# Head outputs of a hybrid decoder step: turned on VectorE and through HBM where they were turned on TensorE

## The chip, the cores and the metric

One core of a Trainium2 chip runs one layer of a decoder step, for a prompt of 1024 tokens (16 meta tokens ahead of it) and 8 single-token samples. The metric is the device time of one execution in microseconds. Of three runs of the kernel before, the median is 1193.43 us (1193.35 to 1194.38).

## What is computed

Cut to what matters, in the reference's names; `_chunked` runs a state through the 16 meta tokens and then through chunks of the sequence:

```python
u = _rms_norm(x, norm_w) @ w_in                       # 1024 -> 8216 columns
q_m, k_m, v_m, o_m, z_m, i_m, f_m, q_g, k_g, v_g, z_g, b_g, a_g = split(u)
(C, n, m), hm = _chunked(_mlstm_chunk, ...)           # 4 mLSTM heads, dk 128, dv 256
ym = _head_rms(hm) * w_mnorm * sigmoid(o_m) * silu(z_m)
qkv = silu(_causal_conv(conv_buf, [q_g, k_g, v_g], conv_w))
S, og = _chunked(_gdn_chunk, ...)                     # 8 gated DeltaNet heads, 128 x 128
yg = (_head_rms(og) * w_gnorm) * silu(z_g)
y = x + concatenate([ym, yg]) @ w_out                 # then a final RMSNorm
```

The same weights serve 8 samples, whose states (C, n, m, S, conv rows) are read, decayed, updated by an outer product and written back. All arithmetic is fp32 in effect: projections split each operand into a high and a low part and add three products.

## The kernel before

**Tiling.** Features lie on the 128 partitions for everything that the projections make (a tile is one head's q, k, v, or one of 8 gate tiles, over 1048 columns of tokens). The input projection takes 56 weight tiles in turn, each over three column blocks of about 350, as 8 x 3 matmuls into a PSUM bank (`pjg`, `pjm`, `pjz`, `pjo`, `pjzm` by group). These matmuls are the filler: 4720 of them, then 672 of the output projection (`op`), in a fixed order.

**Chains.** Beside the filler run the recurrent chains in chunks of 128 tokens: `gdn_chain` for heads 0 to 7, then `mlstm_chain` for heads 0 to 3. A chunk of the mLSTM chain multiplies the state (`mup`, `mnm`), lets VectorE make the next state `C` and the weighted scores `mpm`, turns the next chunk's k and v (`mtp`), and takes some one-element operations for the norm (`mst`, `hst`). Chunk outputs have tokens on the partitions: `oo` (DeltaNet) and `mho` (mLSTM) go to `h_d` in HBM, unscaled.

**Gates.** `gate(kt)` makes one of 16 tiles of the output projection's left side. It loads a head tile `ht` (8 chunks of 128 x 128, tokens on partitions), scales each chunk by the inverse root of the head norm on ScalarE, turns the chunks on TensorE (`hT`, 4 into a PSUM bank), and multiplies them into the gate tile `y` or `mg` on VectorE. DeltaNet's tiles (kt 8 to 15) go to `y_d` and `s_d`, the mLSTM's (0 to 7) are combined with them into `c_d`; the output projection is a Strassen-like scheme of 7 products that reads these as its left sides.

**Samples.** `gdn_sample` takes heads in pairs: states into `db` and `ebuf0`, products on TensorE (`sA`), a turn (`sT`), a row broadcast through HBM into `ebuf1`, decay on GpSimd (128x1024), 8 products on VectorE per head, store. `mlstm_sample` does the same per head (`mqc`, `mqT`, `mms` at the end). When both are done, `db` and the two `ebuf` are reused for the output weights (`in_wo`), summed on GpSimd and split into `owh` and `owl`.

**Order.** `Plan` is an order made while the program is written out: it keeps an estimated clock per engine, takes whichever thread can go on earliest, and otherwise issues filler. `note` holds the estimates of durations, `done`, `read` and `room` those of data, buffers and PSUM banks. Each engine then runs its instructions in exactly this order and waits where something isn't there. All DMAs of this stage are issued by one queue, SP's. Buffers come from rings (`r_kq` 3, `r_v` 4, `r_gm` 3 and later 5, `r_N` 2).

Every instruction is recorded by a helper and so has the line L56; groups are told apart by tile names.

Of the kernel before, what the change touches and what calls it, by code (L numbers as in the profile page):

```python
# [12 lines left out]
F32 = mybir.dt.float32  # L13
# [51 lines left out]
class Plan:  # L65
# [32 lines left out]

    def note(self, eng, op, out, ins, extra, power):
# [197 lines left out]
def hymba_kernel(ctx: ExitStack, tc: tile.TileContext, a: dict, o: dict):  # L297
# [158 lines left out]
    h_d = dr.tile([GH + 2 * MH, P, 8, P], F32, name="h_d")  # L456
# [589 lines left out]
    def gdn_chain(h):  # L1046
# [30 lines left out]
        for c in range(NCH):  # L1077
# [28 lines left out]
            else:  # L1106
                dve.scalar_tensor_tensor(
                    out=Sn, in0=S, scalar=egend[:, c, h : h + 1], in1=up[:, 0:P], op0=ALU.mult, op1=ALU.add)
                oo = w("oo", [258], f"oo{h}_{c}", 3)[:, 0:P]
# [3 lines left out]
                sp.dma_start(h_d[8 + h, :, c - 1, :], oo)  # L1113
# [29 lines left out]
    def query_norms():  # L1143
# [6 lines left out]
        for r in range(4):  # L1150
            rows = slice(32 * r, 32 * r + 32)
            part = pt[rows, 0 : 32 * GH].rearrange("p (h c r) -> p h c r", h=GH, r=4)[:, :, :, r]
            dve.scalar_tensor_tensor(out=hst[rows, MH : MH + GH, :], in0=part, scalar=EPS * MDK, in1=hst[rows, MH : MH + GH, :], op0=ALU.mult, op1=ALU.add)

# [10 lines left out]
    def gdn_sample():  # L1165
# [50 lines left out]
        for i in range(2):  # L1216
            sp.dma_start(sb[i], a["s_S"][i])
        for h in range(0, GH, 2):
# [52 lines left out]
            if h + 2 < GH:  # L1271
                yield plan.read[sb[1].tensor.name]
                sp.dma_start(sb[1], a["s_S"][h + 3])
        op_ = sn[:, 4]
# [11 lines left out]
    def mlstm_jobs(h):  # L1286
# [23 lines left out]
        for part in range(4):  # L1310
# [4 lines left out]
                end=(lambda: done.add(("mP", h))) if part == 3 else None)  # L1315
# [3 lines left out]
    def mlstm_chain(h):  # L1319
        yield lambda: ("mgates",) in done and r_gm.can() and r_N.can()  # L1320
        gi, ew = r_gm.get([NCH, P], f"mgm{h}")
        if h == MH - 1:
            r_gm.idle += [3, 4]
# [14 lines left out]
        yield has("mP", h)  # L1338
        (ki, kq), (v0i, v0), (v1i, v1) = hd["m", h]
        yield v1  # L1340
        qt = wq[:, 1:NCH, :].rearrange("p c t -> p (c t)")
        for c in range(0, SEQ, 512):
            pool.tensor_tensor(out=qt[:, c : c + 512], in0=qt[:, c : c + 512], in1=kq[:, 1, META + c : META + c + 512], op=ALU.mult)
        pre = {}
# [25 lines left out]
        for c in range(NCH):  # L1370
# [18 lines left out]
            if c > 0:  # L1389
                ho = w("oo", [258], f"mho{h}_{c}", 3)  # L1390
                act.copy(ho[:, 0:257], nm[:, 0:257])
                st = w("st", [4], f"mst{h}_{c}")
                jk = w("jm", [256], f"mjk{h}_{c}", bufs=1)
                act.activation(jk, ho[:, 0:256], AF.Square, scale=1.0 / 16, accum_out=st[:, 1:2])
                sp.dma_start(h_d[2 * h : 2 * h + 2, :, c - 1, :].rearrange("i t v -> t i v"), ho[:, 0:256].rearrange("p (i v) -> p i v", i=2))

                def norm(st=st, ho=ho, c=c):
                    dve.tensor_scalar(st[:, 2:3], ho[:, 256:257], -1.0, em[:, c, h : h + 1], op0=ALU.mult, op1=ALU.max)
                    dve.tensor_scalar(st[:, 0:1], ho[:, 256:257], st[:, 2:3], None, op0=ALU.max)
# [17 lines left out]
        r_kq.free(ki)  # L1417
# [5 lines left out]
    def mlstm_sample():  # L1423
# [32 lines left out]
        for h in range(MH):  # L1456
# [14 lines left out]
            for i in range(2):  # L1471
                for b in range(NS):
                    g, j = divmod(b, 4)
                    g = P * (g + 2 * i)
                    pe.matmul(qt[32 * j : 32 * j + 32, g : g + P], qf, sb[i][:, b, :], start=True, stop=True)
            vb = ebuf[1]
# [10 lines left out]
            for i in range(2):  # L1487
# [5 lines left out]
                pool.tensor_tensor(out=s_, in0=s_, in1=decb[:, h].unsqueeze(2).to_broadcast([P, NS, P]), op=ALU.mult)  # L1493
                yield s_
                yield vb
                for b in range(NS):
                    dve.scalar_tensor_tensor(out=s_[:, b], in0=vb[:, b], scalar=kw[:, h, b : b + 1], in1=s_[:, b], op0=ALU.mult, op1=ALU.add)
# [44 lines left out]
    def gate(kt_, wcol):  # L1542

        j = kt_ % 8
        if kt_ >= 8:
            yield lambda: ("mP", MH - 1) in done and ("C", j) in done and ("z", j) in done and (j in slots or (r_kq if j < 6 else r_N).can()) and r_gm.can(2)
            gi, y = r_gm.get([SEQ], f"y{kt_}")
        else:
            yield lambda: ("mC", j // 2) in done and ("y", 8 + j) in done and (j < 2 or ("y", j - 2) in done) and r_gm.can()
# [4 lines left out]
        sp.dma_start(ht, h_d[kt_])  # L1554
        hh = kt_ // 2 if kt_ < 8 else kt_ - 4
        yield has("rs", hh)
        yield rsg[hh][0]
# [3 lines left out]
        yield ht, 1.2  # L1561
# [572 lines left out]
```

## Time and profile before

| what | value |
|---|---|
| median of 3 runs | 1193.43 us |
| profiled execution | 1193.59 us, its span 1191.8 us |
| TensorE matmuls | 1175.5 us busy, 99% |
| VectorE | 880.7 us, 74% |
| ScalarE, GpSimd | 591.0 us, 459.8 us |
| HBM read, written | 107.65 MB, 45.71 MB |
| first and last `hT` | 809.0, 1022.1 us |

Times in rows are microseconds from the span's start, means and durations of single instructions nanoseconds. PE is TensorE, PEld its weight loads, DVE VectorE, ACT ScalarE, POOL GpSimd, SPq the DMA issues of SP's queue. A row of a table of stages gives for each engine its busy time and, in brackets, its instructions. Matmuls overlap in the pipeline: their busy times add up to more than the time from start to start.

### The profile page before, as it was taken

How to read it: one execution, taken by the hardware profiler on the slowest of the kernel's cores; microseconds unless marked ns; L12 is line 12 of the kernel's file. 1: busy time of each engine (PE TensorE's matmuls, PEld its weight loads, DVE VectorE, ACT ScalarE, POOL GpSimd, SP SyncE). 2: the span in 40 equal slices, each digit the busy share in tenths (PEclk: the TensorE clock that was granted, in tenths of full speed). 3: DMA queues.
4: the chain of work that ended last, by engine and by line, in shares of the span. 5: the costliest groups of instructions: out<-in, count | busy, mean ns of one | idle time of the engine just before them, and what ended most of it. 6: DMA issues, size and time to landing. Idle time of an engine off the chain costs nothing.

```text
span 1191.8 us, 22942 instructions
## 1 busy us (share of the span) xinstructions
PE 1175.5 (99%) x8248; PEld 1100.6 (92%) x8248; DVE 880.7 (74%) x2248; ACT 591.0 (50%) x1789; POOL 459.8 (39%) x640
## 2 busy tenths in 40 slices
PE   8999999999999999999999999999999999999997
PEld 7999999999999999999998989999999999876885
DVE  6789788687889888784348666637766765887886
ACT  6554445655565556554444443436444433343544
POOL 3105877837568665847004133140011111440012
PEclk9999999999999999999999999999999999999999
DMA  6032212212211212121122425355798986674342
GB/s 244 19 97 77 86 50 81 89 44 88 79 53 37 92 56 89 38 60 52 50 68 89 141 93 180 99 174 191 243 334 266 322 304 233 214 281 130 108 159 89
DMA packets 87084, 154.86 MB, mean 130 GB/s; under 512 B 26793, under 2 KB 48513, under 8 KB 86970
## 3 DMA queue, kind: packets, MB, share of 16 engines
q1 hardware_dynamic: 86776, 153.23, 38.9%
q8 instruction: 65, 1.06, 0.4%
q14 instruction: 49, 0.40, 0.1%
q10 hardware_dynamic: 194, 0.17, 0.0%
HBM read 107.65 MB, written 45.71 MB: 129 GB/s over the span
## 4 chain that ended last, share of the span: by engine, by line
PE 90%; DVE 5%; DMA 1%; issue 1%; ACT 1%; POOL 1%; SPq 0%; DVEq 0%; POOLq 0%; ACTq 0%
PE pjg L56 23%; PE pjm L56 13%; PE op L56 9%; PE pjo L56 8%; PE pjzm L56 8%; PE pjz L56 7%; PE up L56 4%; PE tp L56 3%; PE sk L56 2%; PE mnm L56 2%; PE mup L56 2%; PE hT L56 1%; PE kk L56 1%; PE mtp L56 1%; PE E L56 1%
## 5 line engine op out<-in xcount | busy, mean ns | idle before, releaser
L56 PE MATMUL pjg<-xht,whg 128*128 128x350 f32 (+6 forms) x624 | 197.4, 323 | 1.0 <-ACT xht L56 1.0
L56 PE MATMUL pjg<-xlt,whg 128*128 128x350 f32 (+6 forms) x624 | 197.4, 323 | 0.0
L56 PE MATMUL pjg<-xht,wlg 128*128 128x350 f32 (+6 forms) x592 | 190.5, 325 | 0.0
L56 POOL TENSOR_TENSOR tmp<-B,E 33x31 f32<-33x31 f32 (+15 forms) x248 | 147.8, 596 | 70.7 <-DMA B<-nd 51.9
L56 POOL TENSOR_TENSOR E<-E,tmp 33x31 f32<-33x31 f32 (+15 forms) x248 | 153.5, 619 | 19.5
L56 PE MATMUL op<-owh,left 128*128 128x512 f32 x448 | 141.6, 395 | 0.7 <-DVE xr L56 0.7
L56 PE MATMUL pjm<-xht,wlm 128*128 128x350 f32 (+2 forms) x384 | 126.4, 329 | 0.6 <-DVE wlm L56 0.6
L56 PE MATMUL pjm<-xht,whm 128*128 128x350 f32 (+2 forms) x384 | 126.5, 329 | 0.0
L56 PE MATMUL pjm<-xlt,whm 128*128 128x350 f32 (+2 forms) x384 | 125.8, 328 | 0.0
L56 PEld LDWEIGHTS pjg<-xht,whg 128*128 128x128 f32 x624 | 116.4, 189 | 1.9 <-issue 1.2
L56 PEld LDWEIGHTS pjg<-xlt,whg 128*128 128x128 f32 x624 | 116.4, 189 | 0.3
L56 PEld LDWEIGHTS pjg<-xht,wlg 128*128 128x128 f32 x592 | 110.9, 189 | 0.5
L56 PEld LDWEIGHTS op<-owh,left 128*128 128x128 f32 x448 | 84.1, 188 | 22.5 <-issue 1.7
L56 DVE SCALAR_TENSOR_TENSOR kq<-cr,prm,kq 128x346 f32<-128x346 f32 (+7 forms) x147 | 94.0, 646 | 11.3 <-ACT kq L56 8.0
L56 POOL TENSOR_TENSOR db<-db,sgb 128x1024 f32<-128x1024 f32 x8 | 15.9, 1985 | 189.9 <-PE mqc L56 121.4
L56 PE MATMUL op<-owl,left 128*128 128x512 f32 x224 | 88.3, 394 | 0.0
L56 PEld LDWEIGHTS pjm<-xht,wlm 128*128 128x128 f32 x384 | 72.5, 189 | 1.4 <-DVE wlm L56 1.2
L56 PEld LDWEIGHTS pjm<-xlt,whm 128*128 128x128 f32 x384 | 72.4, 188 | 0.5 <-issue 0.2
L56 PEld LDWEIGHTS pjm<-xht,whm 128*128 128x128 f32 x384 | 72.3, 188 | 0.4
L56 POOL TENSOR_TENSOR mwq<-mt,mgm 128x384 f32<-128x384 f32 x12 | 10.7, 888 | 140.0 <-DVE mgm L56 140.0
L56 PE MATMUL pjz<-xht,whz 128*128 128x344 f32 x192 | 62.8, 327 | 0.0
L56 ACT COPY cr<-pjg 128x3 f32<-128x3 f32 (+8 forms) x124 | 40.5, 326 | 44.9 <-PE pjg L56 44.6
(368 smaller groups left out, 3211.0 us busy)
## 6 DMA issues: line engine op xcount, KB each, us to landing
wrg<-in_wt SPq DMA_DIRECT2D x23, 512.0 KB
left<-c_d SPq DMA_DIRECT2D x40, 256.0 KB
wrm<-in_wt SPq DMA_DIRECT2D x16, 512.0 KB
ht<-h_d SPq DMA_DIRECT2D x16, 512.0 KB
gm<-rows_d SPq DMA_DIRECT2D x8, 576.0 KB
xt<-in_x_p SPq DMA_DIRECT2D x8, 512.0 KB
wrz<-in_wt SPq DMA_DIRECT2D x8, 512.0 KB
h_d<-oo SPq DMA_DIRECT2D x64, 64.0 KB
```

Source lines behind the costliest of these rows:

```text
L56: r = f(*args, **kw)
```

## The change

1. **Turning.** `oo` goes to a buffer of its own, `o_d`. The new `turns` reads a DeltaNet head back once the DeltaNet norms are there, scales it on ScalarE, and `store` turns it on VectorE in 32x32 blocks (4 instructions of 128x256) and writes it to `h_d` in 4 DMAs of 32 partitions, which put the blocks where a full transpose has them. An mLSTM chunk's output stays in SBUF, in the place of the q and k that it has used up (`mkq`); `stores` takes the inverse roots with a power on GpSimd, scales on ScalarE and calls `store` for the head's two halves. `h_d` now holds scaled tiles with features on partitions, up to an order of columns; `gate` loads one and multiplies it in 4 pieces (128x8x32), without TensorE and without scalings.
2. **Weights.** `mlstm_weights` is a thread of its own: decays and scores' weights of a head are made once the DeltaNet inverses are done and q is there, ahead of the chain.
3. **Samples.** The decay on GpSimd is issued right behind `sA` or `mqc`; the second row broadcast has a buffer (`svb`) of its own; the products yield to other VectorE work after every second one.
4. **Estimates** of VectorE's transpose, reduce and memset in `note` are raised.

```diff
@@ note @@
-            cost = 0.07 + n * (1.04e-3 if len(ins) > ptr + (op[0] == "s") or op == "transpose" else 0.6e-3)
-            cost += 0.06 * ptr
+            if op in ("transpose", "tensor_reduce"):
+                n, cost = free(ins[0]), 1.55e-3
+            else:
+                cost = 1.04e-3 if len(ins) > ptr + (op[0] == "s") else 1.15e-3 if op == "memset" else 0.6e-3
+            cost = 0.07 + n * cost + 0.06 * ptr
...
-    h_d = dr.tile([GH + 2 * MH, P, 8, P], F32, name="h_d")
+    o_d = dr.tile([GH, P, 8, P], F32, name="o_d")
+    h_d = dr.tile([2 * MH + GH, P, D], F32, name="h_d")
...
+    def store(k, o_):
+        yield r_gm.can
+        ti, turn = r_gm.get([D], f"turn{k}")
+        yield plan.read[turn.tensor.name]
+        for b in range(4):
+            yield "dve"
+            blocks = o_.rearrange("p (c b j) -> p b c j", c=8, b=4)[:, b]
+            dve.transpose(turn[:, 256 * b : 256 * b + 256].rearrange("p (c i) -> p c i", c=8), blocks)
+        yield turn
+        for a_ in range(4):
+            sp.dma_start(h_d[k].rearrange("(b j) (a x) -> a j b x", b=4, a=4)[a_], turn[32 * a_ : 32 * a_ + 32].rearrange("p (b x) -> p b x", b=4))
+        r_gm.free(ti)
+        done.add(("H", k))
+    def stores():
+        for h in range(MH):
+            yield has("mC", h)
...
+            pool.tensor_tensor(out=rs, in0=hst[:, h, :], in1=mhalf, op=ALU.pow)
...
+                act.activation(o_, o_, AF.Copy, scale=rs[:, c : c + 1])
+            yield kq
+            for i in range(2):
+                yield from store(2 * h + i, kq[:, i, META:TP])
+            r_kq.free(ki)
@@ gdn_sample, and the like in mlstm_sample @@
+            for i in range(2):
+                pool.tensor_tensor(out=sb[i], in0=sb[i], in1=eg[:, h + i].unsqueeze(2).to_broadcast([P, NS, P]), op=ALU.mult)
             yield at
...
-            vb = ebuf[1]
             for i in range(2):
-                hi, s_ = h + i, sb[i]
-                sp.dma_start(vb, vb_d[8 * hi : 8 * hi + 8].partition_broadcast(P))
-                pool.tensor_tensor(out=s_, in0=s_, in1=eg[:, hi].unsqueeze(2).to_broadcast([P, NS, P]), op=ALU.mult)
+                sp.dma_start(vbs[i], vb_d[8 * (h + i) : 8 * (h + i) + 8].partition_broadcast(P))
...
                 for b in range(NS):
+                    if b % 2 == 0:
+                        yield "dve"
@@ mlstm_chain, now two functions @@
+    def mlstm_weights(h):
+        yield lambda: ("mgates",) in done and ("I", GH - 1) in done
...
+        done.add(("mW", h))
+        hd["w", h] = gi, ew, ni, wq
+    def mlstm_chain(h):
+        yield lambda: ("mP", h) in done and ("mW", h) in done
...
-                ho = w("oo", [258], f"mho{h}_{c}", 3)
-                act.copy(ho[:, 0:257], nm[:, 0:257])
+                ho = kq[:, :, chunk(c)[0] : sum(chunk(c))]
+                act.copy(ho, nm[:, 0:256].rearrange("p (i v) -> p i v", i=2))
...
-                sp.dma_start(h_d[2 * h : 2 * h + 2, :, c - 1, :].rearrange("i t v -> t i v"), ho[:, 0:256].rearrange("p (i v) -> p i v", i=2))
@@ gate @@
-        sp.dma_start(ht, h_d[kt_])
...
-        for c in range(8):
-            act.activation(ht[:, c], ht[:, c], AF.Copy, scale=rsg[hh][0][:, rsg[hh][1], c : c + 1])
+        sp.dma_start(ht.rearrange("p c t -> p (c t)"), h_d[kt_])
...
-        for half in (slice(0, HALF), slice(HALF, SEQ)):
-            yield room("s")
-            pt = pst(f"hT{kt_}_{half.start}")
-            for c in range(4):
-                pe.transpose(pt[:, P * c : P * c + P], ht[:, half.start // P + c, :], ident)
-            dve.scalar_tensor_tensor(out=y[:, half], in0=pt, scalar=wcol, in1=y[:, half], op0=ALU.mult, op1=ALU.mult)
         u = ht.rearrange("p c t -> p (c t)")
+        for a_ in range(4):
+            yield "dve"
+            to = y[:, 0:SEQ].rearrange("p (c a i) -> p a c i", c=8, a=4)[:, a_]
+            dve.scalar_tensor_tensor(out=to, in0=u[:, 256 * a_ : 256 * a_ + 256].rearrange("p (c i) -> p c i", c=8), scalar=wcol, in1=to, op0=ALU.mult, op1=ALU.mult)
@@ head_norms keeps the DeltaNet part @@
+    def turns():
+        for h in range(GH):
+            yield lambda: ("rs", MH + h) in done and ("I", GH - 1) in done and r_gm.can()
...
+            sp.dma_start(t, o_d[h])
...
+                act.activation(t[:, c], t[:, c], AF.Copy, scale=rsg[MH + h][0][:, rsg[MH + h][1], c : c + 1])
+            yield t
+            yield from store(8 + h, t.rearrange("p c t -> p (c t)"))
```

How the instructions stand. First the gate of the first mLSTM tile (`mg`): TensorE and VectorE before.

```order
L56 MATMUL pjo_0_11124<-xht,who_11025 128x344
L56 MATMUL hT_0_11144<-ident,ht_10841 128x128 x4
L56 MATMUL hT_512_11150<-ident,ht_10841 128x128 x4
L56 MATMUL pjo_0_11124<-xlt,who_11025 128x344
...
L56 SCALAR_TENSOR_TENSOR mg_10959<-hT_0_11144,wmq,mg_10959 128x512
L56 SCALAR_TENSOR_TENSOR mg_10959<-hT_512_11150,wmq,mg_10959 128x512
```

And VectorE now, at the same gate; `turn` from `mkq` are the last mLSTM head's two halves, `turn` from `o` the last DeltaNet head:

```order
L56 STREAM_TRANSPOSE turn_11201<-mkq_9932 128x256 x4
L56 SCALAR_TENSOR_TENSOR mg_11076<-ht_11140,wmq,mg_11076 128x8x32 x3
L56 STREAM_TRANSPOSE turn_11276<-mkq_9932 128x256 x3
...
L56 STREAM_TRANSPOSE turn_11276<-mkq_9932 128x256
L56 STREAM_TRANSPOSE turn_11288<-o_11139 128x256 x4
L56 SCALAR_TENSOR_TENSOR mg_11076<-ht_11140,wmq,mg_11076 128x8x32
```

TensorE has no part in a gate any more (the 128 `hT` are its only instructions that go), and the block transposes stand in VectorE's row among the gates' products.

Second, SP's queue at the end of the samples, before (`out_s_C` is a sample state's store, `in_wo` the output weights):

```order
L56 DMA out_s_C<-db 128x1024
L56 DMA wrzm_12768<-in_wt 128x1024
L56 DMA c_d<-ht_12355 128x1024
L56 DMA c_d<-yg_12696 128x1024
L56 DMA out_s_C<-ebuf_101 128x1024
L56 DMA ebuf_101<-in_wo 128x1024
L56 DMA ebuf_102<-in_wo 128x1024
L56 DMA wout_12893<-in_wo 128x1024
L56 DMA ht_12920<-h_d 128x1024
```

and now:

```order
L56 DMA out_s_C<-db 128x1024
L56 DMA c_d<-mg_12686 128x512
L56 DMA yg_12871<-y_d 128x1024
L56 DMA out_s_C<-ebuf_101 128x1024
L56 DMA ebuf_101<-in_wo 128x1024
L56 DMA ebuf_102<-in_wo 128x1024
L56 DMA wout_12951<-in_wo 128x1024
L56 DMA wout_12953<-in_wo 128x1024
L56 DMA wout_12955<-in_wo 128x1024
```

The last projection weight and the last head tile are now loaded ahead of these stores, and six loads of output weights follow each other. Counted in TensorE's order, 196 projection matmuls stood between that last store and the first output matmul, and now 80.

Third, TensorE in the chain of mLSTM head 0 around the first pair of samples (`sA`), before:

```order
L56 MATMUL mup_2_8863<-mkq_7456 128x128
L56 MATMUL sA_8876<-db,skn 32x128 x8
L56 MATMUL sA_8876<-ebuf_101,skn 32x128 x8
L56 MATMUL mup_2_8863<-va_159,mkt_2_8865 128x257
L56 MATMUL mnm_2_8894<-C_1_8857,mwq_8587 128x257
```

and now:

```order
L56 MATMUL sA_8973<-db,skn 32x128 x8
L56 MATMUL sA_8973<-ebuf_101,skn 32x128 x8
L56 MATMUL mup_4_8915<-va_160,mkt_4_8917 128x257
L56 MATMUL mnm_4_8993<-C_3_8905,mwq_7980 128x257
L56 MATMUL mnm_4_8993<-va_160,mpm_4_8920 128x257
```

Pair 0 meets the chain of head 0 two chunks later. The pairs 1 and 2 stood in the chains of heads 1 and 2 in the same way, and now stand behind the end of these chains (72 and 0 projection matmuls behind the last `mup`); pair 3 stood 24 matmuls ahead of the chain of head 3 and now stands 4 ahead of it.

More of the change, by code (lines that the diff above doesn't have):

```diff
@@ L97, in split, with join @@
                 self.read[t.tensor.name, i] = self.read.get(old, 0.0)
+    def join(self, t):
+        name = t.tensor.name
+        del self.parts[name]
+        for times, none in ((self.read, 0.0), (self.done, (0.0, ""))):
+            times[name] = max([times.get(name, none)] + [times.pop(k) for k in list(times) if isinstance(k, tuple) and k[0] == name])
     def note(self, eng, op, out, ins, extra, power):
@@ L1217, in gdn_sample @@
             sp.dma_start(sb[i], a["s_S"][i])
+        yield r_gm.can
+        gi, vb = r_gm.get([NS, P], "svb")
+        yield plan.read[vb.tensor.name]
+        vbs = ebuf[1], vb
         for h in range(0, GH, 2):
@@ L1273, in gdn_sample @@
                 sp.dma_start(sb[1], a["s_S"][h + 3])
+        r_gm.free(gi)
         op_ = sn[:, 4]
@@ L1314, in mlstm_jobs @@
                 evac=lambda part=part: evac_(part),
-                end=(lambda: done.add(("mP", h))) if part == 3 else None)
+                end=(lambda: done.add(("mP", h))) if part == 3 else (lambda: done.add(("mQ", h))) if part == 0 else None)
     vas = [gp.tile([P, 258], F32, name=f"va{i}") for i in range(2)]
-    def mlstm_chain(h):
-        yield lambda: ("mgates",) in done and r_gm.can() and r_N.can()
+    def mlstm_weights(h):
+        yield lambda: ("mgates",) in done and ("I", GH - 1) in done
+        if h == 0:
+            r_gm.idle += [3, 4]
+        yield lambda: r_gm.can() and r_N.can()
         gi, ew = r_gm.get([NCH, P], f"mgm{h}")
-        if h == MH - 1:
-            r_gm.idle += [3, 4]
         ni, wq = r_N.get([NCH, P], f"mwq{h}")
@@ L1337, in mlstm_chain @@
         act.activation(ew, ew, AF.Exp)
-        yield has("mP", h)
-        (ki, kq), (v0i, v0), (v1i, v1) = hd["m", h]
-        yield v1
+        yield has("mQ", h)
+        kq = hd["m", h][0][1]
+        yield kq
         qt = wq[:, 1:NCH, :].rearrange("p c t -> p (c t)")
@@ L1475, in mlstm_sample @@
                     pe.matmul(qt[32 * j : 32 * j + 32, g : g + P], qf, sb[i][:, b, :], start=True, stop=True)
+            for i in range(2):
+                pool.tensor_tensor(out=sb[i], in0=sb[i], in1=decb[:, h].unsqueeze(2).to_broadcast([P, NS, P]), op=ALU.mult)
             vb = ebuf[1]
@@ L1645, in head_norms @@
     def head_norms():
-        for heads in ([("C", h) for h in range(GH)], *([("mC", h)] for h in range(MH))):
-            yield lambda: all(k in done for k in heads)
-            if len(heads) > 1:
-                yield from query_norms()
-            h0 = heads[0][1] if len(heads) == 1 else MH
-            n = slice(h0, h0 + len(heads))
-            yield hst
-            rsqrt_wide(rsg[h0][0], hst[:, n], rst[:, 0 : len(heads)])
-            for i in range(len(heads)):
-                done.add(("rs", h0 + i))
+        yield lambda: all(("C", h) in done for h in range(GH))
+        yield from query_norms()
+        yield hst
+        rsqrt_wide(rsg[MH][0], hst[:, MH : MH + GH], rst)
+        for h in range(GH):
+            done.add(("rs", MH + h))
+    def turns():
+        for h in range(GH):
+            yield lambda: ("rs", MH + h) in done and ("I", GH - 1) in done and r_gm.can()
+            ti, t = r_gm.get([8, P], f"o{h}")
+            yield plan.read[t.tensor.name]
+            sp.dma_start(t, o_d[h])
+            yield rsg[MH + h][0]
+            yield t
+            for c in range(8):
+                yield "act"
+                act.activation(t[:, c], t[:, c], AF.Copy, scale=rsg[MH + h][0][:, rsg[MH + h][1], c : c + 1])
+            yield t
+            yield from store(8 + h, t.rearrange("p c t -> p (c t)"))
+            r_gm.free(ti)
     def gdn_gates():
@@ L2039, in chains, with weights @@
             yield from mlstm_chain(h)
+    def weights():
+        for h in range(MH):
+            yield from mlstm_weights(h)
     def samples():
@@ L2054, in hymba_kernel @@
     plan.add(chains(), 0.3)
-    for t in (late_evacs(), each(gdn_merge), each(gdn_inverse), each(gdn_prep), each(gdn_decay), in_turn(tails), in_turn(convs), head_norms(), gdn_gates(), weight_loads(), right_sums(), right_splits(), left_loads(), left_splits(), residual(), sample_rows()):
+    for t in (late_evacs(), each(gdn_merge), each(gdn_inverse), each(gdn_prep), each(gdn_decay), in_turn(tails), in_turn(convs), head_norms(), stores(), weights(), turns(), gdn_gates(), weight_loads(), right_sums(), right_splits(), left_loads(), left_splits(), residual(), sample_rows()):
         plan.add(t)
```

42 lines of the change are left out of this document (27 added, 15 removed).

## The prediction

> **What bounds the kernel now.** I read the page first, then a table of stages, then TensorE's own waits, then single stretches of the timeline.
>
> ```profile
> span 1191.8 us, 22942 instructions
> PE 1175.5 (99%) x8248; PEld 1100.6 (92%) x8248; DVE 880.7 (74%) x2248; ACT 591.0 (50%) x1789; POOL 459.8 (39%) x640
> ...
> PE 90%; DVE 5%; DMA 1%; issue 1%; ACT 1%; POOL 1%; SPq 0%; DVEq 0%; POOLq 0%; ACTq 0%
> ```
> ```profile
> core 0: us, PE busy (x) PEld busy (x) DVE busy (x) ACT busy (x) POOL busy (x), PEclk, DMA share, GB/s
> 0.00:640.00 640.00, 634.64 (x4919) 610.51 (x4920) 491.64 (x1327) 352.49 (x1145) 350.33 (x566) 1.00 0.24 74
> 640.00:800.00 160.00, 157.18 (x1065) 148.33 (x1065) 98.96 (x317) 66.39 (x204) 46.54 (x42) 1.00 0.41 137
> 800.00:1000.00 200.00, 200.00 (x1406) 194.69 (x1406) 138.90 (x377) 91.97 (x279) 19.90 (x10) 1.00 0.78 267
> 1000.00:1192.00 192.00, 183.64 (x865) 147.11 (x863) 151.22 (x228) 80.12 (x162) 43.01 (x24) 0.99 0.50 168
> ```
> The first fence is the page, the second the stages. TensorE is busy 1175.5 of 1191.8 us, 90% of the chain that ended last is its own, and its clock is full. From 800 to 1000 us, where the gates are made, it has no idle time at all. A busy share alone could hide waits, so I ask what it waited for:
>
> ```profile
> engine line waited for: us in total, times, longest us
> PE mup L56 <- DVE mpm L56: 2.4, 3, 0.8
> ...
> PE mup L56 <- ACT va L56: 1.0, 1, 1.0
> ...
> PE up L56 <- DVE R L56: 0.4, 1, 0.4
> ```
> The longest entry is 2.4 us, and no wait is over 1.0. So a microsecond of TensorE work taken out is nearly a microsecond of the run, as long as nothing else becomes late; and time on any other engine is free as long as it stays hidden.
>
> **The change, part by part.** The sum is made against the profiled execution, 1193.59 us (span 1191.8), which is 0.16 over the median of 1193.43.
>
> *TensorE's transposes go.* Sixteen head tiles are no longer turned on TensorE, 128 transposes in all:
>
> ```profile
> L56 PE MATMUL hT<-ident,ht 128*128 128x128 f32 x128 | 17.8, 275 | 0.0
> ...
> 842.07 0.32 PE L56 MATMUL pjo<-xht,who 128*128 128x344 f32 x1
> 842.23 1.03 PE L56 MATMUL hT<-ident,ht 128*128 128x128 f32 x8
> 843.02 0.40 PE L56 MATMUL pjo<-xlt,who 128*128 128x344 f32 x1
> 843.26 0.32 PE L56 MATMUL pjo<-xht,wlo 128*128 128x344 f32 x1
> ```
> Durations overlap in the pipeline, so I count from start to start. Eight transposes hold TensorE from 842.23 to 843.02, 0.79 us; the projection matmul behind them then takes 0.24 to the next start where the one before took 0.16, so 0.08 more. 16 groups x 0.87 = **13.9 us**. The ends are 16 x 0.79 = 12.6 and the busy sum of 17.8; I take 13.9 because starts are what the next instruction sees.
>
> *VectorE turns the tiles.* Of what it gets and loses, these are the nearest rows:
>
> ```profile
> L56 DVE STREAM_TRANSPOSE srow<-srow 128x256 f32<-128x256 f32 x32 | 13.9, 435 | 0.6 <-ACT srow L56 0.4
> L56 DVE SCALAR_TENSOR_TENSOR y<-hT,wgh,y 128x512 f32<-128x512 f32 x16 | 11.4, 747 | 8.7 <-PE hT L56 8.3
> L56 DVE SCALAR_TENSOR_TENSOR mg<-to,mg 128x344 f32<-128x344 f32 x24 | 16.5, 688 | 0.8
> L56 DVE SCALAR_TENSOR_TENSOR db<-ebuf,skn,db 128x128 f32<-128x128 f32 x32 | 8.8, 347 | 0.3 <-issue 0.3
> L56 DVE TENSOR_SCALAR rst<-rst 128x8 f32<-128x8 f32 x12 | 2.1, 171 | 0.4
> ...
> L56 POOL TENSOR_TENSOR kap<-kap,phalf 128x9 f32<-128x9 f32 x8 | 14.7, 1837 | 109.7 <-DVE kap L56 109.7
> ```
> 64 block transposes of 128x256 cost 64 x 0.435 = 27.8. The gate product was 32 x 0.747 = 23.9 and becomes 64 of 256 elements, between 0.347 (128 elements) and 0.688 (344): on the line between them 0.55, so 35.2. Of the mLSTM heads' inverse roots 52 small operations go, 52 x 0.17 = 8.8. Together VectorE gets 27.8 + 35.2 - 23.9 - 8.8 = 30.3 us more. Nearly all stands between 640 and 1000 us, where it is busy 99.0 + 138.9 of 360; with 30 more and 14 us less time that is 268 of 346, 78%. I cost it at nothing: the projection matmuls cover it. Uncovered, it would be up to 30.
>
> The Trainium skill speaks against this part: VectorE: DVE Perf Modes, section Rules for kernel authors, sends a 128x128 transpose to TensorE where PSUM will do as a target, since VectorE turns 32x32 blocks only. The trace bears out the price: 0.435 for two such tiles against 0.20 on TensorE. By the rule the sum would go up by as much of the 27.8 as is uncovered; by the rows of the stages it goes down by 13.9.
>
> *ScalarE, GpSimd.* The 128 scalings become 64 of the same size and 32 of twice it, plus 32 copies of one element, under an engine busy 92 of 200. The inverse roots become four powers on GpSimd, up to 1.8 us each (kap, a power of 9 elements, is the nearest row), with nothing on TensorE behind them. Both: nothing.
>
> *mLSTM weights apart, samples decayed sooner.* This touches the 3.4 us of waits above. Where they come from is seen at one of them:
>
> ```profile
> 650.78 1.91 POOL L56 TENSOR_TENSOR ebuf<-ebuf,sgb 128x1024 f32<-128x1024 f32 x1
> ...
> 650.79 1.92 DVE L56 TENSOR_TENSOR mst<-mst 128x1 f32<-128x1 f32 x1
> 652.92 0.29 DVE L56 TENSOR_TENSOR mpm<-mup,mgm 128x128 f32<-128x128 f32 x1
> ...
> 653.36 0.67 PE L56 MATMUL mup<-va,mkt 128*128 128x257 f32 x2 [0.80 <-DVE mpm L56]
> ...
> L56 DVE TENSOR_TENSOR mst<-mst x32: 159/160/1920, 650.8 to 828.7; 128x1 f32<-128x1 f32 x32
> ```
> GpSimd decays a sample state for 1.91 us; a one-element product on VectorE, 0.160 as a rule, lasts 1.92 beside it; the next chunk's weights (mpm) come late, and TensorE waits 0.80. This happens three times, once for each pair of sample heads that is decayed inside a chain. In the new order pairs 2 and 3 are decayed after the chains of heads 1 and 2 have ended, and only the first and the last pair still meet a chain (0 and 3). I take 1.6 off (two of the three) and 0.2 of the start of chain 0, whose weights are now ready before: **1.8 us**; the ends are 0 and 3.4. The Trainium skill says the same of it (SBUF — State Buffer, section Who interferes with whom): a VectorE instruction with two SBUF inputs and a GpSimd instruction that reads SBUF exclude each other for a whole instruction. The trace agrees with 1.92 beside 1.91. The rule also speaks against the new gate products, which read SBUF twice where one input was in PSUM. GpSimd is busy 19.9 of 200 us there, so a tenth of 64 products would lose about 1 us each, 6 us of VectorE; under 78% load that adds nothing to the sum by rule or row.
>
> *The output weights come later.* The last sample store now stands 80 projection matmuls ahead of the first matmul of the output projection, where it stood 196 ahead, and the loads of the output weights reuse its buffers.
>
> ```profile
> 985.20 0.34 SPq L56 DMA_DIRECT2D out_s_C<-ebuf  x1
> 989.15 0.81 SPq L56 DMA_DIRECT2D ebuf<-in_wo  x2
> ...
> 994.34 2.41 POOL L56 TENSOR_TENSOR db<-ebuf,ebuf 128x1024 f32<-128x1024 f32 x1 [19.81 <-DMA ebuf<-in_wo]
> ...
> L56 ACT CAST owh<-db x4: 611/618/624, 1007.9 to 1019.7; 128x512 fp32r<-128x512 f32 x4
> L56 DVE TENSOR_TENSOR owl<-db,owh x4: 679/684/693, 1008.6 to 1022.0; 128x512 fp32r<-128x512 f32 x4
> ```
> From the store's issue to the sum's end is 996.75 - 985.20 = 11.55; a cast and a low part, 0.62 + 0.68, and three hand-overs of 0.15 (mpm's end at 653.21 to mup at 653.36 above) make 13.3. Eighty projection matmuls at 0.16 last 12.8. I take the difference, **+0.5**, with the ends 0 and 6 (a landing twice as long, 994.34 - 989.15 = 5.2 more).
>
> *DMA.* Eight loads of 512 KB and 32 more stores' worth of 128 KB (64 against 32) are 8.4 MB more, and 40 more issues on SP of about 0.4 each (0.81 for two above), 16 us of a queue with gaps. By the order some 6.3 MB falls before the gates' stage, where the engines are busy 0.41: nothing. The remaining 2.1 MB falls after 800 us.
>
> *VectorE's estimates.* They move instructions of the DeltaNet stage; TensorE waits there 0.4 for R and has nothing else to gain. New small waits from the new order: **+1.0**, ends 0 and 4, by the sizes in TensorE's list.
>
> Sum: 1193.59 - 13.9 - 1.8 + 0.5 + 1.0 = **1179.4 us**, 1.2% less.
>
> **Rivals.** *Part of it is lost to late transfers.* For it:
>
> ```profile
> 850.00:900.00 50.00, 50.00 (x382) 49.05 (x381) 34.10 (x81) 21.14 (x63) 4.58 (x3) 1.00 0.92 312
> 900.00:950.00 50.00, 50.00 (x354) 48.55 (x353) 33.83 (x77) 23.32 (x70) 7.80 (x4) 1.00 0.87 296
> ```
> The gates' stage runs the DMA engines at 0.92, and now gets 2.1 MB more (6 us at 267/0.78 = 342 GB/s) and 14 us less time: 156 + 6 of 186, 0.87 on average, over 1 in the stretch that was 0.92. Gates and sample states then slip by some 8 us: 1187. Against it: TensorE has no wait on a transfer in its list now.
>
> *Slower.* The sample chain sits on that same queue, and behind it the output weights. If its loads slip, the store with 80 matmuls behind it goes out late, and all of the slip is idle time at the first output matmul. It decides from 16.4 us of slip on (1195.8 - 1179.4); with 20, 1199. For it: the place of the store. Against it: each head's sample states have 20 to 45 matmuls between load and use in both orders.
>
> *No change.* The new work of VectorE holds up chain and gates by as much as TensorE gains: 14 of its 30 us uncovered, 1193; all 30 uncovered would be 1209. Against it: 78%, which leaves VectorE some 78 us idle in these stages. The skill's rule on transposes, above, points this way.
>
> *More.* All 3.4 us of waits go and nothing new comes: 1176.3, and 1174 if the transposes are worth 16.
>
> **How the numbers follow.** Forecast (1176 to 1184) 0.65; more than that 0.06; part lost 0.17; no change 0.05; slower 0.07. A difference under 0.2% (1191.0 to 1195.8) can't be told from none. Of the part lost 0.01 ends there: faster 0.87, same 0.06, slower 0.07. The range 1174 to 1188 takes in the bounds of the terms and most of the part lost.
>
> **What the profile would show.** No hT rows and about 1161 us of TensorE busy; 64 more VectorE transposes near 0.435 and gate products near 0.55; mup waiting for mpm about twice; op waiting for owh or owl under 2 us; DMA near 0.87 between the gates' first load and the last pjzm. The forecast is wrong if TensorE shows idle time of several us before mqc, pjzm or the first op, or if its filler matmuls stretch.

## The result, and the profile after

The changed kernel takes 1180.09 us in the median of four runs (1178.65 to 1181.36), the kernel before 1193.7 beside it. The ratio is 0.9882 with an interval of 0.9867 to 0.9897: 14.1 us less, where 14.2 were forecast. The profiled execution is the longest of the four (1181.36, span 1179.6). Two single executions in the experiments below, of 2634 us (without TensorE's transposes) and 1643 us (the kernel before with new estimates), lie far off the others of their kernels and are left out of their ratios. First its page and its table of stages, in the columns of the prediction's.

```profile
span 1179.6 us, 22735 instructions
PE 1163.7 (99%) x8120; PEld 1090.1 (92%) x8120; DVE 892.9 (76%) x2292; ACT 587.2 (50%) x1789; POOL 464.4 (39%) x644
```
```profile
core 0: us, PE busy (x) PEld busy (x) DVE busy (x) ACT busy (x) POOL busy (x), PEclk, DMA share, GB/s
0.00:640.00 640.00, 634.12 (x4901) 610.48 (x4902) 483.75 (x1304) 354.37 (x1144) 359.05 (x577) 0.99 0.24 75
640.00:800.00 160.00, 159.41 (x1086) 151.25 (x1084) 106.10 (x348) 89.52 (x301) 38.23 (x32) 1.00 0.51 164
800.00:1000.00 200.00, 200.00 (x1384) 195.44 (x1373) 155.55 (x419) 68.25 (x197) 24.62 (x12) 1.00 0.84 293
1000.00:1179.60 179.60, 170.13 (x765) 132.98 (x764) 147.48 (x222) 75.08 (x147) 42.47 (x25) 0.98 0.51 170
```
The 128 transposes are gone (8248 to 8120 matmuls), and from 640 to 1000 us TensorE idles 0.6 us. VectorE has 106.1 + 155.6 of these 360 us, 73%. So far this is the forecast. But the clock column shows 0.99 and 0.98 in two stages where the kernel before had it at 1.00 and 0.99 (there only at its tail). TensorE's waits say where to look:

```profile
engine line waited for: us in total, times, longest us
PE up L56 <- ACT vt L56: 2.1, 1, 2.1
PE op L56 <- DVE xr L56: 2.0, 1, 2.0
...
PE mup L56 <- ACT srow L56: 0.6, 1, 0.6
```
The list no longer names mpm (2.4) and va (1.0), the waits of the mLSTM chains. The 0.6 put down to srow is one more of the same kind, as its stretch of the timeline shows:

```profile
659.26 1.91 POOL L56 TENSOR_TENSOR ebuf<-ebuf,sgb 128x1024 f32<-128x1024 f32 x1
...
659.39 1.80 DVE L56 SCALAR_TENSOR_TENSOR hst<-mst 128x1 f32<-128x1 f32 x1
...
661.11 0.28 DVE L56 TENSOR_TENSOR mpm<-mup,mgm 128x128 f32<-128x128 f32 x1
...
661.54 0.67 PE L56 MATMUL mup<-va,mkt 128*128 128x257 f32 x2 [0.59 <-ACT srow L56]
```
A one-element operation that takes 0.160 us as a rule lasts 1.80 beside GpSimd's decay of a sample state, mpm comes late, and mup starts 0.15 us behind it.

Two waits of 2 us have come, one in the DeltaNet stage (405.8 to 407.9 us), one in the output projection (1051.5 to 1053.5). The next table, by stretches of 3.41 us around each of them, shows what follows these two:

```profile
core 0: us, PE busy (x) PEld busy (x) DVE busy (x) ACT busy (x) POOL busy (x), PEclk, DMA share, GB/s
...
404.72:408.13 3.41, 1.29 (x9) 0.92 (x8) 2.90 (x7) 2.26 (x7) 3.02 (x6) 1.00 0.43 110
408.13:411.54 3.41, 3.41 (x13) 2.61 (x12) 2.19 (x8) 1.49 (x6) 3.10 (x5) 0.50 0.36 116
411.54:414.96 3.42, 3.42 (x14) 3.42 (x15) 1.42 (x5) 0.52 (x2) 3.03 (x6) 0.50 0.03 5
414.96:418.37 3.41, 3.41 (x26) 3.41 (x25) 1.89 (x6) 2.74 (x9) 3.10 (x5) 1.00 0.00 0
1049.83:1053.25 3.42, 1.64 (x7) 0.73 (x5) 3.42 (x7) 1.65 (x3) 1.46 (x1) 1.00 0.38 137
1053.25:1056.66 3.41, 3.15 (x7) 2.48 (x8) 3.41 (x7) 0.62 (x1) 0.91 (x1) 0.50 0.12 19
```
Behind each wait the granted clock is 0.50, for 6.83 and for 3.41 us: 13 and 14 matmuls in a stretch where the next, at 1.00, has 26. Counted from start to start against the medians of the same pairs of instructions, the two stretches cost 3.3 and 1.5 us on top of the waits. In this execution a wait of 2 us is thus worth 3.5 to 5.4.

What the new instructions of VectorE cost, by groups and shapes:

```profile
L56 DVE SCALAR_TENSOR_TENSOR mg<-ht,wmq,mg 128x256 f32<-128x256 f32 x32 | 18.8, 642 | 0.1
...
L56 DVE SCALAR_TENSOR_TENSOR y<-ht,wgh,y 128x256 f32<-128x256 f32 x32 | 13.7, 478 | 6.6 <-DMA ht<-h_d 6.6
...
L56 DVE STREAM_TRANSPOSE turn<-o 128x256 f32<-128x256 f32 x32 | 11.6, 413 | 7.9 <-ACT o L56 4.8 <-DMA h_d<-turn 3.1
L56 DVE STREAM_TRANSPOSE turn<-mkq 128x256 f32<-128x256 f32 x32 | 11.5, 414 | 5.1 <-ACT mkq L56 2.9 <-DMA y_d<-y 1.5 <-DVE wlm L56 0.6
```

### The profile page after: what moved, and what is told of

Its sections match the earlier page's. It is cut to its first block, busy times and chain, and to the rows that moved or that the text cites. A ratio compares the mean times of both kernels' runs of the same rounds, so it can differ in the third digit from the quotient of the medians.

```text
span 1179.6 us, 22735 instructions
## 1 busy us (share of the span) xinstructions
PE 1163.7 (99%) x8120; PEld 1090.1 (92%) x8120; DVE 892.9 (76%) x2292; ACT 587.2 (50%) x1789; POOL 464.4 (39%) x644
## 4 chain that ended last, share of the span: by engine, by line
PE 93%; DVE 4%; issue 1%; ACT 1%; POOL 0%; DVEq 0%; POOLq 0%; ACTq 0%
PE pjg L56 23%; PE pjm L56 16%; PE op L56 9%; PE pjz L56 8%; PE pjo L56 8%; PE pjzm L56 7%; PE up L56 4%; PE tp L56 3%; PE sk L56 2%; PE mnm L56 2%; PE mup L56 2%; PE kk L56 1%; DVE owl L56 1%; PE mtp L56 1%; DVE left L56 1%
## 5 line engine op out<-in xcount | busy, mean ns | idle before, releaser
L56 PE MATMUL pjz<-xht,wlz 128*128 128x344 f32 x192 | 62.6, 326 | 0.0
```

The lines of the kernel that those rows point to most:

```text
L56: r = f(*args, **kw)
```

## The experiments

Each ratio is to the kernel before on the same chip; differences in microseconds are worked out from the ratios at 1193.5.

### What TensorE's transposes were worth: the kernel before without them

```diff
-        for half in (slice(0, HALF), slice(HALF, SEQ)):
-            yield room("s")
-            pt = pst(f"hT{kt_}_{half.start}")
-            for c in range(4):
-                pe.transpose(pt[:, P * c : P * c + P], ht[:, half.start // P + c, :], ident)
-            dve.scalar_tensor_tensor(out=y[:, half], in0=pt, ...)
+            yield "dve"
+            dve.scalar_tensor_tensor(out=y[:, half], in0=u[:, half], ...)
```

> The kernel before, with the 128 transposes on TensorE left out: the gate products read the loaded tile as it lies, so that the outputs are multiplied unturned. It leaves out the turning of the outputs. Nothing is added on VectorE or the DMA queues. Theory: TensorE's term alone, 16 x 0.87 = 13.9 us: 1193.7 - 13.9 = 1179.8 us. Ends 12.6 (1181.1) and 17.8 (1175.9). If TensorE now reaches the wait for xr in the output stage 0.87 us sooner and waits 1.6 instead of 0.7 us there, 0.9 of it is lost, and 1.7 more if the clock is halved for 3.4 us behind it: up to 1182.4. Rival: something else becomes late without the transposes, over 1184.

Measured: ratio 0.9894 (0.9879 to 0.9908), 12.7 us less, 1180.9 by the ratio against 1179.8. Its list of waits:

```profile
PE mup L56 <- DVE mpm L56: 2.3, 3, 0.8
PE pjo L56 <- DVE mg L56: 1.4, 1, 1.4
```
The chain waits stay, as they must, and a wait of 1.4 us for mg and one of 0.8 for a gate tile are new; 3.41 us at half clock stand at 640.5 us. With these 2.2 us added back, the 12.7 become an estimate of 14.9 for the transposes alone (1.5 more where the clock falls, as it did in this profiled execution, the longest of the four). The theory holds.

### The second and third part alone

The kernel before with `mlstm_weights` as a thread, the decays issued behind `sA` and `mqc`, and `svb`:

```diff
-    def mlstm_chain(h):
-        yield lambda: ("mgates",) in done and r_gm.can() and r_N.can()
+    def mlstm_weights(h):
+        yield lambda: ("mgates",) in done and ("I", GH - 1) in done
...
+            for i in range(2):
+                pool.tensor_tensor(out=sb[i], in0=sb[i], in1=decb[:, h].unsqueeze(2).to_broadcast([P, NS, P]), op=ALU.mult)
```

> The kernel before, with only the weights of the mLSTM heads made apart and the sample states decayed sooner (second and third part of the change alone; outputs still turned on TensorE). The prediction's term: -1.8 us, ends 0 and -3.4: 1193.7 - 1.8 = 1191.9. Rival: as the changed kernel's list of TensorE's waits has no mpm, va or wlm left (2.4 + 1.0 + 0.6 us before, 0.6 for srow now), these two parts are worth 3.4 us by themselves: 1190.3. Second rival: they are worth nothing alone, and the waits went because the outputs no longer pass ScalarE and TensorE: 1193.7.

Measured: ratio 0.9984 (0.9976 to 0.9993), 1.9 us less; 1191.75 us in the median. That is the prediction's term to a tenth, but not for its reason:

```profile
PE mup L56 <- DVE mpm L56: 2.3, 4, 0.8
```
The decays were to free the waits for mpm, and these still add up to 2.3, though they are no longer the same ones. Two of them (0.75 and 0.79) come as before from an mst of 1.92 us beside a sample decay, where there were three. The next (0.58) comes from the weights' own work: at 754.21 us a wlm takes 1.53 us beside a product of mwq on GpSimd (1.27 us). What went is the wait for va at the start of the first chain (1.0) and the one for wlm (0.6, with one of 0.6 for mv in its place); the list is 1.5 us shorter in all.

### The estimates: taken from the changed kernel, given to the kernel before

```diff
-            if op in ("transpose", "tensor_reduce"):
-                n, cost = free(ins[0]), 1.55e-3
-            else:
-                cost = 1.04e-3 if len(ins) > ptr + (op[0] == "s") else 1.15e-3 if op == "memset" else 0.6e-3
-            cost = 0.07 + n * cost + 0.06 * ptr
+            cost = 0.07 + n * (1.04e-3 if len(ins) > ptr + (op[0] == "s") or op == "transpose" else 0.6e-3)
+            cost += 0.06 * ptr
```

> The changed kernel with the planner's VectorE estimates as they were before (the fourth part of the change undone, the other three kept). In the profile of the changed kernel TensorE waits 2.12 us for ScalarE's vt at 405.8 us, and right behind it the granted clock is 0.5 for 6.83 us, which costs half of that, 3.4 us. Theory: the new estimates set the order in which vt stands behind the query squares; with the old ones the wait and the halved clock behind it are gone, 1180.1 - 2.1 - 3.4 = 1174.6 us (1173 to 1176.5), and no record of 0.5 stands near 400 us. Rival 1: the wait comes from the other parts (sample states decayed sooner, buffers taken by the sample stage): it stays, 1180 us. Rival 2: the old estimates price 64 block transposes and the reduces wrong, and waits come elsewhere: over 1182 us.

> The kernel before with the new VectorE estimates alone (the fourth part of the change without the other three). With the old estimates the changed kernel took 1186.0 instead of 1180.1 us, so this part is worth 6 us there, where the prediction had nothing. Theory: what it is worth is the place of the output weights behind the last sample store (with the old estimates TensorE waited 5.0 us for owh and owl, with the new ones not at all); the kernel before has 196 matmuls of cover there and no such wait, so alone it gains nothing and brings the wait for vt with the halved clock behind it: 1193.5 + 2.1 + 3.4 = 1199 us (1193.5 if the wait for vt doesn't arise). Rival: the new estimates are better everywhere, and worth about 6 us here too: 1187.5.

> The kernel before with the second, third and fourth part of the change (mLSTM weights apart, samples decayed sooner, new VectorE estimates), the outputs still turned on TensorE: the changed kernel without its first part. Theory: without the first part the estimates only bring the wait for vt; 1191.75 (second and third part alone) + 3.3 (what the estimates cost the kernel before) = 1195 us, so that turning on VectorE is worth 15 us with the new estimates and 5.7 us (1191.75 - 1186.05) with the old. Rival: the estimates gain 6 us whatever stands beside them, 1186 us, and the first part is worth 6 us in both.

| outputs turned on | weights apart, samples sooner | estimates | ratio to before (interval) | us |
|---|---|---|---|---|
| TensorE | no | old | 1 | 0 |
| TensorE | no | new | 1.0031 (1.002 to 1.0042) | +3.7 |
| TensorE | yes | old | 0.9984 (0.9976 to 0.9993) | -1.9 |
| TensorE | yes | new | 0.998 (0.9971 to 0.999) | -2.4 |
| VectorE | yes | old | 0.9932 (0.992 to 0.9944) | -8.1 |
| VectorE | yes | new | 0.9882 (0.9867 to 0.9897) | -14.1 |

My theory for the first run fell and its second rival held: without the new estimates the changed kernel is not faster by 5 us but slower by 6.0, with waits elsewhere. The second run's theory held (no gain alone, a wait for vt), though 3.7 us is less than the 5.5 it named. For the third neither theory nor rival did: its 1190.7 us lie between the 1195 and the 1186 expected. What the estimates are worth hangs on what stands beside them: +3.7, -0.5 and -6.0 us in the three pairs of the table. The waits tell where. The changed kernel with the old estimates:

```profile
PE op L56 <- DVE owl L56: 3.5, 2, 3.3
PE op L56 <- ACT owh L56: 1.5, 1, 1.5
PE mup L56 <- DVE mpm L56: 1.3, 2, 0.7
```
The wait for vt is gone, as I had expected, but TensorE waits 5.0 us for the output weights, with a stretch at half clock behind it. The last sample store and the first output matmul, in the timeline of this kernel and then of the changed one:

```profile
993.57 0.34 SPq L56 DMA_DIRECT2D out_s_C<-ebuf  x1
...
1005.21 0.49 PE L56 MATMUL op<-owh,left 128*128 128x512 f32 x1 [1.54 <-ACT owh L56]
```
```profile
989.39 0.34 SPq L56 DMA_DIRECT2D out_s_C<-ebuf  x1
...
1004.36 0.39 PE L56 MATMUL op<-owh,left 128*128 128x512 f32 x1
```
With the new estimates the store leaves 4.2 us sooner, and 92 projection matmuls start between the two in time (80 was the count in TensorE's order); with the old there are 60 and a wait. The prediction's chain of load, sum, cast and low part was 13.3 us; 92 matmuls at 0.16 are 14.7, 60 are 9.6. The old formula prices a block transpose of 256 elements at 0.07 + 256 x 0.00104 = 0.34 us, the new one at 0.47; the group above has 0.41. With 64 of them in the way of the sample chain the plan runs ahead of the engine by 64 x 0.07 = 4.5 us. That this shortfall moves the store is argued from the plan's rules, not shown by a run of its own; nor was it run which of the corrected prices (transposes, reduces, memsets) does it.

On the other side of the ledger, the kernel before with the new estimates (one profiled execution, of 1194.05 us):

```profile
PE mup L56 <- DVE mpm L56: 4.3, 4, 1.9
PE up L56 <- ACT vt L56: 2.1, 1, 2.1
```

> A look at the kernel before with the new VectorE estimates alone, which took 3.3 us more than the kernel before. Theory: TensorE waits 1.3 to 2.1 us for vt in the DeltaNet stage, with 3.4 or 6.8 us at half clock behind it (1.7 or 3.4 us), and no other wait is new. Rival: the 3.3 us lie in the mLSTM or the output stage.

The wait for vt comes with the estimates, in every kernel of the table that has the new ones and in none that has the old. The 1.9 us more for mpm I had not expected: it is a single wait at 812.37 us, behind the decays of the fourth pair of sample heads (807.79 and 809.66 us), beside which a wlzm takes 2.03 us and an mst 0.99. This one execution kept its clock and is 0.6 us over the kernel before; the timed ones have a mean clock of 0.996 on average, the kernel before beside them 0.9985, and 0.0025 of 1195 us is 3.0 of the 3.7. With the second and third part beside them mpm is gone from the list, and vt is the only wait over 1.0; one of 0.6 for srow is left, beside a decay at 655.57 us as in the changed kernel. So the decays stand clear of the chains, but for this one, only where the estimates and the two parts come together; whether both parts are needed for it was not run.

### Is VectorE's time free? The turns issued twice, all of them and every second one

```diff
             dve.transpose(turn[:, 256 * b : 256 * b + 256].rearrange("p (c i) -> p c i", c=8), blocks)
+            nc.vector.transpose(turn[:, 256 * b : 256 * b + 256].rearrange("p (c i) -> p c i", c=8), blocks)
```

The second kernel has the added line for odd `b` alone.

> The changed kernel with every one of the 64 block transposes on VectorE issued twice (the second writes the same again), the order of all else unchanged. VectorE gets 64 x 0.435 = 27.8 us more of the stage where it has the most to do. Theory: VectorE's time there is hidden under the projection matmuls: 1180.1 us within 1.5. Rival: it is at its limit, and what is added shows by half or whole: 1194 to 1208. Between them (1183 to 1188): single chains wait, not the engine as a whole.

> The changed kernel with every second of the 64 block transposes issued twice: 13.9 us more on VectorE, half of what the doubled transposes added, which cost 14 us. Theory: there is some slack left, and time is lost where single loads, splits and sums of the sample states come late by more than their cover; half the dose is hidden for the most part: 1180 to 1184 us. Rival: VectorE's time shows at a fixed rate, 0.5 us for 1 us: 1187 us, and then the 30 us of the change itself weren't free either.

Measured: all twice 0.9997 (0.9981 to 1.0012), so 13.7 us over the changed kernel, about half of the 28 added, the rival's lower end; every second one 0.992 (0.9905 to 0.9935), 4.5 over it, at the edge of the theory's range. My theory that there was room for twice the work fell; the rival's fixed rate asks for 1187 us in the second run, whose interval is 1182.2 to 1185.7: it is out, if not by much (4.5 for the first 14 us, 9.2 for the next). The waits with all twice:

```profile
PE pjzm L56 <- DVE wlzm L56: 4.4, 1, 4.4
PE op L56 <- DVE xr L56: 2.3, 2, 2.0
PE up L56 <- ACT vt L56: 2.1, 1, 2.1
PE sA L56 <- DMA ebuf<-in_s_S: 1.9, 1, 1.9
PE sA L56 <- DMA db<-in_s_S: 1.2, 1, 1.2
```
TensorE does not wait for VectorE all along. It waits a few times for single things that came after their cover had run out: the low part of a gate weight (wlzm), the reload of sample states (sA). Behind the reload stand 10.24 us at half clock and behind wlzm 6.83, which costs about as much again as the waits. This execution is the longest of twelve. VectorE still has idle time in this stage, 267.5 of 360 us busy:

```profile
640.00:1000.00 360.00, 350.76 (x2351) 335.33 (x2350) 267.51 (x793) 154.88 (x491) 60.56 (x42) 0.98 0.66 223
```
What runs out first is the lead of the one item that is due, not the engine.

### The two new waits: a tile for the squares, and sums handed out sooner

The row of ScalarE ahead of vt, in the changed kernel's timeline:

```profile
406.09 0.42 ACT L56 ACTIVATE srow<-kq 128x256 f32<-128x256 f32 x1 [0.99 <-DVE srow L56]
406.41 0.47 ACT L56 ACTIVATE cr<-kq 128x336 f32<-128x336 f32 x1
407.03 0.42 ACT L56 ACTIVATE srow<-kq 128x256 f32<-128x256 f32 x1 [0.15 <-DVE srow L56]
407.36 0.28 ACT L56 ACTIVATE gs<-z,wgh 128x8 f32<-128x8 f32 x1
407.55 0.34 ACT L56 ACTIVATE vt<-tp,kap 16x128 f32<-16x128 f32 x1
```
ScalarE stands still until VectorE has turned the squares of the block before, since both blocks use one tile, and vt is queued behind. The first kernel gives every second block its own tile. The second does that too and takes 2 us of slack out of the hand-over of the residual sums.

```diff
-            sq, turned = srow[:, 0 : 2 * P], srow[:, 2 * P : 4 * P]
+            sq, turned = (sqrow if i % 2 else srow[:, 0 : 2 * P]), srow[:, 2 * P : 4 * P]
```
```diff
             x_ = xr[c, t][:, HALF * h : HALF * h + HALF]
-            yield x_
+            yield x_, 0.5
```

> The changed kernel, with a tile of its own for every second block of query squares, so that ScalarE's next square doesn't wait until VectorE has turned the one before. In the profile of the changed kernel ScalarE stands 0.99 and 0.15 us for that, with vt queued behind it, and TensorE waits 2.12 us for vt. Theory: the wait for vt shrinks to about 1.0 us and the clock behind it stays full: 1180.1 - 1.1 - 3.4 = 1175.6 us. Rival: the wait comes from VectorE's delay, not from ScalarE's row, and stays: 1180 us.

> The kernel with the tile of its own for the squares, and besides the sums into the residual rows handed to VectorE 2 us sooner after their loads are due (0.5 instead of 2.5 us of slack in the planner). It aims at TensorE's wait of 2.04 us for xr in the output stage and the 3.4 us at half clock behind it. Theory: VectorE's order sets that wait; it falls under 1 us and the clock stays full: 3 us less than with the squares alone, 1172.5 us. Rival: the loads of the residual rows set it (the transfer engines are busy without a gap from 1028 to 1048 us), VectorE then only waits for them, with other work queued behind: no gain, or 1 to 2 us more than with the squares alone.

Measured: the tile alone 0.9859 (0.9844 to 0.9874), 1177.37 us, 2.7 less than the changed kernel; both 0.9831 (0.9819 to 0.9844), 1173.38 us, another 3.3 less. The waits of the kernel with both:

```profile
PE up L56 <- ACT vt L56: 1.2, 1, 1.2
PE rise L56 <- DVE ones L56: 1.0, 1, 1.0
PE pjg L56 <- ACT xht L56: 1.0, 1, 1.0
```
The wait for vt falls from 2.1 to 1.2 and the one for xr leaves the list; no stretch at half clock is left ahead of the tail. Both theories hold for the waits; the first gained less than the 4.5 expected, most likely because the profile it was drawn from lost more clock than the other executions of its kernel: the four have mean clocks of 0.994 (the profiled one), 0.996, 0.996 and 0.998, with spans of 1179.6, 1177.7, 1178.9 and 1176.9 us. The rival, that the loads of the residual rows set the second wait, is out, since the wait went when only the slack of these sums was changed. This kernel is the fastest here, 20.2 us under the one before.

### When does the clock halve?

A stage behind the end of that kernel, in which TensorE's idle times are set:

```diff
+    for i, n in enumerate([steps[(i * 5) % 32] for i in range(32)]):
+        for _ in range(32 + i * 3 % 8):
+            pe.matmul(pt, wh[:, 0, 0:P], wl[:, 0], start=True, stop=True)
+        while n > 0:
+            m = min(n, 512)
+            dve.tensor_tensor(out=x_[:, 0:m], in0=x_[:, 0:m], in1=pt[:, 0:m], op=ADD)
+            n -= m
```

> The same kernel with a stage added behind its end: 32 bursts of 32 to 39 matmuls of 128x512, each of which must wait until VectorE has read the bank that the burst before filled; VectorE reads 256 to 2560 elements (0.4 to 3.5 us), four times each, so that TensorE's idle times go from some 0.8 to 4 us at different places of the clock's raster. Its time says nothing. Theory: the clock is set in windows of 3.41 us on a fixed raster; a window with 1.7 us of idle time or more is followed by one at 0.5, one with 1.4 or less isn't. So waits of 1.0 us never halve the clock, those of 2.1 us do so only where one window holds most of them, and those of 3 us and more always. Rival: the length of the wait alone decides, wherever it lies: one bound between 1.0 and 2.0 us. Second rival: what was seen at 408 and 1053 us has another cause, and waits of 2 us leave the clock full here.

The drops of the clock start on one raster, that is, a whole number of equal stretches (windows) apart: 1223.49 and 1486.32, the first and the last but one of them, lie 77.0 stretches of 3.413 us apart, and so do 408.13 and 1053.25 of the changed kernel (189.0). Three places, cut along the raster, in the columns of the tables above:

```profile
1274.69:1278.11 3.42, 1.47 (x7) 0.96 (x6) 1.79 (x3) 0.00 (x0) 0.00 (x0) 1.00 0.00 0
1278.11:1281.52 3.41, 3.41 (x10) 2.63 (x9) 0.00 (x0) 0.00 (x0) 0.00 (x0) 0.50 0.00 0
...
1349.79:1353.20 3.41, 1.58 (x7) 0.96 (x6) 1.73 (x3) 0.00 (x0) 0.00 (x0) 1.00 0.00 0
1353.20:1356.62 3.42, 3.03 (x13) 2.54 (x14) 0.33 (x1) 0.00 (x0) 0.00 (x0) 1.00 0.00 0
1428.29:1431.71 3.42, 1.61 (x8) 0.99 (x6) 1.70 (x3) 0.00 (x0) 0.00 (x0) 1.00 0.00 0
1431.71:1435.12 3.41, 2.28 (x10) 1.90 (x11) 1.04 (x2) 0.00 (x0) 0.00 (x0) 1.00 0.01 2
```
The first holds the whole of a wait of 1.96 us and is followed by 0.50. The second has 1.83 idle, most of a wait of 2.22, and is not. The third is the first part of a wait of 2.94, which the raster cuts into 1.81 and 1.13: no drop. Over this stage, of the windows at full clock, every one with 1.95 us or more of idle time was followed by 0.50 (11 of 11) and none with 1.83 or less. So the windows of the theory hold, but not its bound of 1.7. The length of the wait alone does not decide (waits of 2.22 and 2.94 us left the clock full, one of 1.96 did not), so the first rival is out, and the second with it. In the kernels themselves the windows with 2.03 us or more dropped too, but below that the bound is less sharp: windows with 1.71 and 1.78 idle were followed by a drop, two with 1.72 were not, and one with 1.10 was (the one ahead of 640.5 us above). What counts beside idle time there is open, and so is how long a drop lasts: here a window at half clock with 1.44 idle was followed by another, and in the changed kernel so was one without idle time (408.13 us).

## Why the prediction came out right

**TensorE's transposes, -13.9.** Right. Summed from start to start, the 128 took 13.75 us before. The prediction's 0.08 for the matmul behind them shows at the 13 projection matmuls that followed a group directly, 1.1 us in all: 14.8 in the changed kernel, 12.7 to 14.9 alone.

**The chains' waits, -1.8.** Too small, and the mechanism was only half of it. The list had 4.4 us before (mpm, va, wlm, R) and has 0.8 after (srow, wv): -3.6. In the changed kernel it went much as forecast: the first pair of sample heads still meets a chain (the 0.6 put down to srow), and the others cost nothing, the fourth included, which was to meet one too. But the two parts to which the prediction gave this are worth 1.9 alone, with two of the three waits beside decays still there; these go only with the new estimates. That 1.9 met 1.8 is luck. And the wait for va, of which 0.2 was taken off, went whole (1.0).

**The output weights, +0.5.** Near (no wait came), but for an incomplete reason: with the old estimates it is 5.0 us of waiting, near the upper end of 6. The rival for "slower" had its place here, and a part of the change that I had set aside kept it away.

**VectorE's estimates, nothing.** This step failed. "They move instructions of the DeltaNet stage" overlooked that the first part adds 64 of the very instructions whose price is corrected, and that the plan orders the sample chain with them. Beside the other three parts the estimates are worth -6.0. It did not show in the total, since the prediction took the changed kernel's order of instructions, which has the new prices in it, and counted the 80 matmuls of cover there.

**New small waits, +1.0.** This term was mis-sized: 2.1 for vt and 1.3 more for xr, and the clock took 4.8 on top, 8.2 in the profiled execution. I had read "no wait is over 1.0" as a list of sizes, when it was also what kept the clock at full speed.

**VectorE's 30 us, at nothing.** Right, but with less room than 78% suggested: 14 us more cost 4.5. The turns were 0.41 and the products 0.48 and 0.64, near the 0.435 and 0.55 taken. (Three of the 32 products of 0.64 ran beside GpSimd operations and took 2.0 to 2.6 us; the other 29 have a mean of 0.48. These three lost 5.3 us together, where the prediction reckoned with 6 in all.) VectorE as a whole rose by 12.2, not 30.3. Most of the difference is in the products of a pair's second sample head, before and after:

```profile
L56 DVE SCALAR_TENSOR_TENSOR ebuf<-ebuf,skn,ebuf 128x128 f32<-128x128 f32 x32 | 20.7, 715 | 4.8 <-DMA ebuf<-vb_d 4.8
```
```profile
L56 DVE SCALAR_TENSOR_TENSOR ebuf<-svb,skn,ebuf 128x128 f32<-128x128 f32 x32 | 8.9, 341 | 0.0
```
That is 11.8 us of VectorE, which the prediction did not count. Before, 17 of these 32 ran while GpSimd made the mLSTM weights (mgm and mwq): the one at 684.91 us, for example, took 1.17 us beside an mgm of 1.01, where the 15 with GpSimd idle took 0.34 to 0.35. In the changed kernel none of them meets that work, and two of the first head's products do (1.10 and 0.91 us).

**DMA.** 0.84 between 800 and 1000 us, forecast 0.87 on average, and no wait on a transfer: the rival of late transfers stays out.

In the profiled execution: -14.8 - 3.6 + 3.4 + 4.8 = -10.2, of 12.2 us that its span is shorter; the other 2.0 I could not place. So the main term was right, but that the sum met the time within 1 us is luck: terms were off by up to 7.2 us and largely cancelled. Chains, transposes and the part not placed gave more than forecast, the two waits and the clock took it back.

## What to carry to other kernels

Where an order is planned from estimates, an edit that adds instructions and an edit that prices them are one change: cost them together, at the place where the plan's lead is thinnest, not where the priced instruction stands today. An engine that is 75% busy is not free for the rest: ask of each item that TensorE needs how many matmuls lie between its start and its use. And on a TensorE that hardly ever idles, one wait of 2 us can cost more than four of 0.5: look at the clock column behind every wait that a change makes longer.

## What the runs showed of the hardware

I had not expected that 2 us of waiting could halve TensorE's clock. In these runs it is granted in windows of 3.41 us on a raster that the program does not set, and a window at full clock with 1.95 us of idle time or more was followed each time by one (sometimes two or three: 6.83, 10.24 us) at 0.50. The raster lies differently in each execution, so the same wait for vt of 2.1 us costs 5.4 us in the changed kernel's profile and only itself in that of the kernel with the second to fourth part, where the raster cuts it and no window has more than 1.51 idle. Runs of one kernel then spread: of the twelve of that last kernel, the four with a mean clock of 0.995 to 0.996 took 1192.4 to 1193.7 us, the eight with 0.998 to 0.999 took 1188.9 to 1191.3. With both waits mended the four runs lie within 1.2 us. The Trainium skill (TensorE: Matmul & The Clock Gate, section What's actually happening) has the window of 3.4 us and says that it runs freely; these traces agree, with 3.413. Its section Why this matters for your kernels advises against idle gaps over about 3 us between bursts of matmuls; here gaps of 1.95 us were enough when they fell into one window.
